# Inverses of 32x32 blocks in a decoder step: rows split by parity over the partitions, 8x8 blocks apart

## The chip, the core and the metric

The kernel runs on one core of one Trainium2 chip. The metric is the device time of one execution in microseconds (us). The core has five engines with queues of their own, each of which starts its instructions in order: TensorE (PE, with its weight load PEld), VectorE (DVE), ScalarE (ACT), GpSimd (POOL), and SyncE (SP), which in this kernel issues nearly all DMAs. An instruction that waits holds up whatever stands behind it on its engine.

## The reference

One decoder layer is applied to a prompt of 512 tokens and to 8 sampled sequences of 8 tokens (64 tokens more; 576 columns in all). Two token mixers share one input projection: an SSD mixer and an RWKV-7 mixer with 16 heads of 64. The change lies in the second. What it computes, per head and token:

```python
def step(s, inp):
    r_t, w_t, k_t, v_t, kk_t, a_t = inp
    s_kk = jnp.einsum('bhvk,bhk->bhv', s, kk_t)
    s = (s * w_t[:, :, None, :] - s_kk[..., None] * (kk_t * a_t)[:, :, None, :]
         + v_t[..., None] * k_t[:, :, None, :])
    return s, jnp.einsum('bhvk,bhk->bhv', s, r_t)
```

After the mixers come the output projection, a SwiGLU block, a per-layer embedding and norms. All of it is large matrix products with 576 columns.

## The kernel before

**The chunked form.** The recurrence is evaluated in chunks of 64 tokens: 8 chunks of the prompt (g = 1 to 8), and one chunk g = 0 that holds the 64 sampled tokens as 8 independent blocks of 8. Inside a chunk the delta rule needs the inverse of a unit lower triangular 64x64 matrix (stored transposed, so upper) for each head. The 16 heads are worked in four quarters of four heads (`jj` = 0, 1 and `e` = 0, 1), one quarter after the other.

**One quarter** goes through these steps, each a function: `prep` (decay, keys; elementwise work on DVE, ACT and POOL), `start_states` and `gram` (products of keys, masked; the strictly triangular part is kept in the tile `Lst`), `bonus`, `decayed`, `solve`, `combine`, `chain` (a serial pass over the chunks, with the state handed from one to the next) and `head_norm`.

**`solve`** inverts the two 32x32 diagonal blocks (`z` = 0, 1) of every 64x64 matrix. Two blocks, two heads `e`, 9 chunks and two `jj` make 72 blocks. They go from `Lst` to DRAM (`Ld`, line 669) and come back with one block on each of 72 partitions (`L`, line 672). DVE starts `Tt` as identity minus `L` (lines 674 and 675). Then 30 steps, each one product into `tmp` (line 681) and one subtraction (line 683), substitute column after column over all rows that are reached so far. A transposed copy (line 684) of the first half goes to `Ad`, and `Tt` to `Td` (lines 685 and 686).

**`combine`** loads `Td` into `TT` and `Ad` into `AA`, and makes the off-diagonal 32x32 block with two rounds of 64 small matmuls (lines 705 and 719). `chain` uses `TT`.

**What sets the order.** The functions are written one after the other, and a scheduler then gives each engine one fixed order by its own estimates. It lays independent work of other stages into the long serial ones: the input projections ("fills", lines 228 to 230; each loads weights as `raw` tiles in a ring of three, line 206, and splits them into `whi` on ACT and `wlo` on POOL and DVE in turn), and the chain of the previous quarter, which runs beside the solve of the next. So a solve has beside it on DVE the elementwise part of projections (lines 375 to 378), every other `wlo` (line 213) and the steps of the previous quarter's chain (lines 799, 812, 838).

Of the kernel before, what the change touches and what calls it, by code (L numbers as in the profile page):

```python
# [75 lines left out]
def hybrid_step(ctx, tc, A):  # L76
    nc = tc.nc
# [14 lines left out]
    def act(out, in_, func=AF.Copy, scale=1.0, bias=0.0):
        return S.activation(out, in_, func, bias=bias, scale=scale)  # L93
# [559 lines left out]
    def decayed(s):  # L653

        for jj in jj2:
            t = s.BK[jj][:, 1:9].rearrange("p g a t -> p g (a t)")
            G.tensor_tensor(t, t, s.PC[:, jj, 8:16].unsqueeze(2).to_broadcast([P, 8, P]), ALU.mult)

    def solve(s):

# [1 line left out]
        Ld = dp.tile([2, 2, 18, 32, 32], F32, tag=f"Ld{q}", name=f"Ld{q}")
        s.Td = dp.tile([2, 2, 18, 32, 32], F32, tag=f"Td{q}", name=f"Td{q}")
        s.Ad = dp.tile([2, 18, 32, 32], F32, tag=f"Ad{q}", name=f"Ad{q}")
        NB = 72
        for z in range(2):
            for e in range(2):
                r0 = e * 64 + z * 32
                nc.sync.dma_start(Ld[z, e].rearrange("g s t -> s g t"),
                                  s.Lst[r0:r0 + 32, :, :, z * 32:z * 32 + 32].rearrange("s g j t -> s (g j) t"))  # L670
        L = sp.tile([NB, 32, 32], F32, tag="L", name=nm("L"))
        nc.sync.dma_start(L[:], Ld[:].rearrange("z e g s t -> (z e g) s t"))
        Tt = s2.tile([NB, 32, 32], F32, tag="Tt", name=nm("Tt"))
        V.tensor_scalar(Tt[:], L[:], -1.0, None, ALU.mult)
        V.tensor_tensor(Tt[:].rearrange("p s t -> p (s t)")[:, 0:1024:33],
                        Tt[:].rearrange("p s t -> p (s t)")[:, 0:1024:33], ones[0:NB, 0:32], ALU.add)
        tmp = s2.tile([NB, 256], F32, tag="tmp", name=nm("tmp"))
        for jx in range(1, 31):
            n = 31 - jx
            o = tmp[:, 0:jx * n].rearrange("p (s t) -> p s t", s=jx)  # L680
            V.tensor_tensor(o, L[:, jx:jx + 1, jx + 1:32].to_broadcast([NB, jx, n]),  # L681
                            Tt[:, 0:jx, jx:jx + 1].to_broadcast([NB, jx, n]), ALU.mult)
            V.tensor_tensor(Tt[:, 0:jx, jx + 1:32], Tt[:, 0:jx, jx + 1:32], o, ALU.subtract)  # L683
        V.tensor_copy(L[0:36], Tt[0:36].rearrange("p s t -> p t s"))
        nc.sync.dma_start(s.Td[:].rearrange("z e g s t -> (z e g) s t"), Tt[:])
        nc.sync.dma_start(s.Ad[:].rearrange("e g s t -> (e g) s t"), L[0:36])

    def combine(s):

        TT = s.TT = inverses[s.q % 2]  # L690
        AA = s2.tile([P, 9, 2, 32], F32, tag="AA", name=nm("AA"))
        for e in range(2):
            for z in range(2):
                r0 = e * 64 + z * 32
                nc.sync.dma_start(TT[r0:r0 + 32, :, :, z * 32:z * 32 + 32].rearrange("s g j t -> s (g j) t"),
                                  s.Td[z, e].rearrange("g s t -> s g t"))
# [4 lines left out]
        for g in range(1, 9):
            for jj in jj2:
                for e in range(2):
                    lo_, hi_ = e * 64, e * 64 + 32
                    marks["c", s.q] = T.matmul(Wv[hi_:hi_ + 32, g - 1, jj, :], s.Lst[lo_:lo_ + 32, g, jj, 32:64],
                                               AA[lo_:lo_ + 32, g, jj, :], start=True, stop=True)
        for e in range(2):
            hi_ = e * 64 + 32
            if e:
                act(AA[hi_:hi_ + 32, 1:9], Wv[hi_:hi_ + 32], scale=-1.0)  # L710
            else:
                V.tensor_scalar(AA[hi_:hi_ + 32, 1:9], Wv[hi_:hi_ + 32], -1.0, None, ALU.mult)
# [1034 lines left out]
```

## Time and profile before

| | before |
|---|---|
| median of 3 runs | 1334.37 us (1331.13 to 1338.24) |
| the profiled execution | 1329.48 us, of which 1327.7 us are the span from its first to its last instruction |
| mean granted TensorE clock | 0.951 |
| instructions | 26629 |
| HBM read, written | 106.10 MB, 27.75 MB |

A row of a group of instructions gives the line, engine and operation, the tiles written and read, the shapes, the count, the busy time in us and the mean of one in ns, then the idle time of the engine ahead of them and what ended it. A row of the timeline gives start and duration in us. A row of a stretch of time gives the busy us of PE, PEld, DVE, ACT and POOL, each with its number of instructions, then the granted clock, the DMA share and GB/s. Line numbers are those of the kernel before; after the diff they stand 37 higher from `combine` on.

### The profile page before, as it was taken

To read this page: it belongs to the slowest core of one execution; us is meant where nothing else is said; L and a number is where in the kernel's file an instruction comes from. 1 tells how busy PE (TensorE), PEld (TensorE's weight loads), DVE (VectorE), ACT (ScalarE), POOL (GpSimd) and SP (SyncE) were. 2 spreads that over 40 slices of the span, in tenths; PEclk is the share of its full clock that TensorE was granted. 3 is DMA by queue.
4 is the path that set the end of the run, shared out by engine and by line. 5 is a ranking of instruction groups with operands and counts; after the bars stand their busy time and mean duration, and the time that the engine had idled before them with its cause. 6 is when DMAs were issued, how large, how long until landed. Compare 5 with 4: busy or idle time off the path is not lost.

```text
span 1327.7 us, 26629 instructions
## 1 busy us (share of the span) xinstructions
PE 1224.9 (92%) x10429; PEld 1125.1 (85%) x10429; DVE 885.8 (67%) x1569; ACT 632.0 (48%) x1274; POOL 615.4 (46%) x584
## 2 busy tenths in 40 slices
PE   6897899999989978899989989999999999999997
PEld 5786797889968966788769878999999999999996
DVE  6649665878696876953456576858895138883464
ACT  6565436543654374343444364455553225553363
POOL 5426513642265136122445665647565345654642
PEclk9898999799978979979989989999999999999998
DMA  5322241334232322353454541253342224424322
GB/s 167 127 65 72 78 116 54 98 96 119 73 103 79 83 72 78 103 180 106 132 182 131 201 151 59 78 161 106 98 113 89 81 83 114 116 66 136 99 89 72
DMA packets 96764, 140.29 MB, mean 106 GB/s; under 512 B 34960, under 2 KB 39312, under 8 KB 96640
## 3 DMA queue, kind: packets, MB, share of 16 engines
q1 hardware_dynamic: 93760, 133.36, 32.6%
q0 software_dynamic: 2304, 4.72, 2.1%
q8 instruction: 82, 1.34, 0.4%
q10 hardware_dynamic: 576, 0.52, 0.1%
q14 instruction: 42, 0.34, 0.1%
HBM read 106.10 MB, written 27.75 MB: 101 GB/s over the span
## 4 chain that ended last, share of the span: by engine, by line
PE 58%; DVE 19%; ACT 6%; issue 6%; DMA 4%; POOL 3%; SPq 0%; DVEq 0%; ACTq 0%; POOLq 0%
PE lin L241 12%; PE lin L1432 11%; PE lin L228 6%; PE lin L230 6%; PE lin L229 6%; DVE h L402 2%; DVE wl L191 1%; DVE Tt L683 1%; DVE tmp L681 1%; DVE wlo L213 1%; PE lin L1577 1%; PE lin L1578 1%; PE lin L1579 1%; DVE suv L838 1%; DMA raw<-wts 1%
## 5 line engine op out<-in xcount | busy, mean ns | idle before, releaser
L213 POOL TENSOR_TENSOR wlo<-raw,whi 128x512 fp32r<-128x512 f32 (+1 forms) x92 | 125.8, 1368 | 303.6 <-ACT whi L93 235.0
L228 PE MATMUL lin<-xhi,whi 128*128 128x288 f32 (+1 forms) x784 | 242.1, 309 | 2.8 <-ACT whi L93 2.2
L230 PE MATMUL lin<-xhi,wlo 128*128 128x288 f32 (+1 forms) x784 | 240.2, 307 | 4.0 <-POOL wlo L213 2.3
L229 PE MATMUL lin<-xlo,whi 128*128 128x288 f32 (+1 forms) x784 | 239.6, 306 | 1.2 <-POOL xlo L191 1.1
L93 ACT ACTIVATE whi<-raw 128x512 fp32r<-128x512 f32 (+1 forms) x200 | 123.2, 616 | 211.0 <-PE lin L241 90.0
L228 PEld LDWEIGHTS lin<-xhi,whi 128*128 128x128 f32 (+1 forms) x784 | 149.5, 191 | 10.1 <-ACT whi L93 2.6
L230 PEld LDWEIGHTS lin<-xhi,wlo 128*128 128x128 f32 (+1 forms) x784 | 149.4, 191 | 7.9 <-POOL wlo L213 2.7
L229 PEld LDWEIGHTS lin<-xlo,whi 128*128 128x128 f32 (+1 forms) x784 | 149.4, 191 | 6.5 <-POOL xlo L191 2.4
L213 DVE TENSOR_TENSOR wlo<-raw,whi 128x512 fp32r<-128x512 f32 (+1 forms) x108 | 82.1, 761 | 74.2 <-PE lin L241 36.0
L1432 PE MATMUL lin<-T,wh 128*128 128x288 f32 x576 | 87.3, 296 | 2.0 <-DVE e L1477 1.3
L1432 PEld LDWEIGHTS lin<-T,wh 128*128 128x128 f32 x576 | 80.0, 189 | 3.2 <-DVE e L1477 1.6
L93 ACT ACTIVATE wh<-raw 128x512 fp32r<-128x512 f32 x72 | 45.1, 628 | 52.5 <-PE lin L1432 35.4
L191 POOL TENSOR_TENSOR wl<-raw,wh 128x512 fp32r<-128x512 f32 x36 | 57.3, 1592 | 11.7 <-ACT wh L93 6.2
L191 DVE TENSOR_TENSOR wl<-sw,wh 128x512 fp32r<-128x512 f32 x53 | 49.9, 941 | 9.3 <-ACT wh L93 5.2
L241 PE MATMUL lin<-ah,whi 128*128 128x288 f32 x352 | 54.7, 294 | 0.0
L241 PE MATMUL lin<-al,whi 128*128 128x288 f32 x352 | 54.4, 294 | 0.0
L241 PE MATMUL lin<-ah,wlo 128*128 128x288 f32 x352 | 54.2, 294 | 0.0
L681 DVE TENSOR_TENSOR tmp<-L,Tt 72x30 f32<-72x30 f32 (+14 forms) x120 | 49.9, 416 | 3.2
L1432 PE MATMUL lin<-T,wl 128*128 128x288 f32 x288 | 49.8, 297 | 0.6 <-DVE wl L191 0.6
L241 PEld LDWEIGHTS lin<-ah,whi 128*128 128x128 f32 x352 | 49.3, 188 | 0.0
L241 PEld LDWEIGHTS lin<-al,whi 128*128 128x128 f32 x352 | 49.2, 188 | 0.0
L241 PEld LDWEIGHTS lin<-ah,wlo 128*128 128x128 f32 x352 | 49.2, 188 | 0.0
(437 smaller groups left out, 3265.7 us busy)
## 6 DMA issues: line engine op xcount, KB each, us to landing
raw<-wts SPq DMA_DIRECT2D x271, 256.0 KB, 2.6
S<-s_wkv SPq DMA_DIRECT2D x8, 512.0 KB, 5.1
hd<-s_ssm SPq DMA_DIRECT2D x8, 512.0 KB, 4.6
o_ssm_s<-hd SPq DMA_DIRECT2D x8, 512.0 KB, 2.8
xbc_d<-E SPq DMA_DIRECT2D x12, 288.0 KB, 2.1
x<-xT SPq DMA_DIRECT2D x8, 288.0 KB
gate_d<-g SPq DMA_DIRECT2D x8, 288.0 KB, 2.5
bv_d<-rw SPq DMA_DIRECT2D x8, 288.0 KB
```

What stands on the lines that cost most here:

```text
L93: return S.activation(out, in_, func, bias=bias, scale=scale)
L191: eng.tensor_tensor(lo, src, hi.bitcast(F32), ALU.subtract)
L213: eng.tensor_tensor(lo[:, 0:n], raw[:, 0:n], hi[:, 0:n].bitcast(F32), ALU.subtract)
L228: T.matmul(ps[:, a:b], whi, xhi[:, a:b], start=first, stop=False)
L229: T.matmul(ps[:, a:b], whi, xlo[:, a:b], start=False, stop=False)
L230: T.matmul(ps[:, a:b], wlo, xhi[:, a:b], start=False, stop=last)
L241: T.matmul(ps[:, a:e], (hi, lo)[p][:, i * P:(i + 1) * P], xs[k + i][q][:, a:e], start=n == k + i == 0, stop=n == 2 and k + i == nk - 1, sk ...
L402: V.scalar_tensor_tensor(h[:], E[:, i:i + 600], w(i), h[:], ALU.mult, ALU.add)
L681: V.tensor_tensor(o, L[:, jx:jx + 1, jx + 1:32].to_broadcast([NB, jx, n]), Tt[:, 0:jx, jx:jx + 1].to_broadcast([NB, jx, n]), ALU.mult)
L683: V.tensor_tensor(Tt[:, 0:jx, jx + 1:32], Tt[:, 0:jx, jx + 1:32], o, ALU.subtract)
L838: V.scalar_tensor_tensor(dst, sv[h, jj, 0, e], PC[h, jj, 7 + g:8 + g], dw[h, jj], ALU.mult, ALU.add)
L1432: T.matmul(ps, (hi, lo)[p][:, k * P:(k + 1) * P], OPS[n][k][q], start=first and p == q == k == 0, stop=p == 1 and k == 3, skip_group_check ...
```

## The change

It is confined to `solve`, the loads of `combine` and a new function.

- The 64 blocks of the prompt's chunks go to the 128 partitions twice, by four DMAs instead of one: partitions 0 to 63 hold the even rows of the 64 inverses, partitions 64 to 127 the odd ones. Each half uses the rows 0, 2, 4, ... of its tile `Tt`. GpSimd sets `Tt` to zero and writes the ones of the diagonal; the identity-minus-`L` step on DVE is gone. The substitution has 31 steps instead of 30, and step `jx` works on `jx // 2 + 1` rows instead of `jx`, on 128 partitions instead of 72.
- The transposed copy is made in two halves, one on DVE and one on ACT, and ACT moves the odd rows beside the even ones before `Td` is written by two DMAs.
- The sampled chunk's blocks are block diagonal with blocks of 8x8. Their 32 blocks of 8x8 are loaded by 8 small DMAs, inverted on GpSimd by 14 instructions (`small_blocks`), and written into `Td` by 8 small DMAs. The rest of those places in `Td` is set to zero once, at the start, by 8 DMAs.
- A solve then issues 33 DMAs instead of 13.

```diff
+    inverse_d = [dp.tile([2, 18, 2, 32, 32], F32, tag=f"Td{q}", name=f"Td{q}") for q in range(4)]
+    zero = sp.tile([8, 1024], F32, tag="L", name=nm("zero"))
+    G.memset(zero[:], 0.0)
+    for d in inverse_d:
+        for z in range(2):
+            nc.sync.dma_start(d[z, 0:2].rearrange("g e s t -> (g e) (s t)"), zero[0:4])
...
-        L = sp.tile([NB, 32, 32], F32, tag="L", name=nm("L"))
-        nc.sync.dma_start(L[:], Ld[:].rearrange("z e g s t -> (z e g) s t"))
-        Tt = s2.tile([NB, 32, 32], F32, tag="Tt", name=nm("Tt"))
-        V.tensor_scalar(Tt[:], L[:], -1.0, None, ALU.mult)
-        V.tensor_tensor(Tt[:].rearrange("p s t -> p (s t)")[:, 0:1024:33],
-                        Tt[:].rearrange("p s t -> p (s t)")[:, 0:1024:33], ones[0:NB, 0:32], ALU.add)
-        tmp = s2.tile([NB, 256], F32, tag="tmp", name=nm("tmp"))
-        for jx in range(1, 31):
-            n = 31 - jx
-            o = tmp[:, 0:jx * n].rearrange("p (s t) -> p s t", s=jx)
-            V.tensor_tensor(o, L[:, jx:jx + 1, jx + 1:32].to_broadcast([NB, jx, n]),
-                            Tt[:, 0:jx, jx:jx + 1].to_broadcast([NB, jx, n]), ALU.mult)
-            V.tensor_tensor(Tt[:, 0:jx, jx + 1:32], Tt[:, 0:jx, jx + 1:32], o, ALU.subtract)
-        V.tensor_copy(L[0:36], Tt[0:36].rearrange("p s t -> p t s"))
-        nc.sync.dma_start(s.Td[:].rearrange("z e g s t -> (z e g) s t"), Tt[:])
-        nc.sync.dma_start(s.Ad[:].rearrange("e g s t -> (e g) s t"), L[0:36])
+        Tt = s2.tile([P, 32, 32], F32, tag="Tt", name=nm("Tt"))
+        flat = Tt.rearrange("p s t -> p (s t)")
+        G.memset(Tt[:, 0:32:2], 0.0)
+        for h in range(2):
+            G.memset(flat[H[h], h:1024:66], 1.0)
+        L = sp.tile([P, 32, 32], F32, tag="L", name=nm("L"))
+        for z in range(2):
+            for h in range(2):
+                r0 = h * 64 + z * 32
+                nc.sync.dma_start(L[r0:r0 + 32], Ld[z, 2:18].rearrange("g e s t -> (g e) s t"))
+        small_blocks(Ld, s.Td)
+        tmp = s2.tile([P, 256], F32, tag="tmp", name=nm("tmp"))
+        for jx in range(31):
+            m, n = jx // 2 + 1, 31 - jx
+            o = tmp[:, 0:m * n].rearrange("p (s t) -> p s t", s=m)
+            V.tensor_tensor(o, L[:, jx:jx + 1, jx + 1:32].to_broadcast([P, m, n]),
+                            Tt[:, 0:2 * m:2, jx:jx + 1].to_broadcast([P, m, n]), ALU.mult)
+            V.tensor_tensor(Tt[:, 0:2 * m:2, jx + 1:32], Tt[:, 0:2 * m:2, jx + 1:32], o, ALU.subtract)
+        V.tensor_copy(L[0:32, :, 0:32:2], Tt[0:32, 0:32:2].rearrange("p s t -> p t s"))
+        act(L[0:32, :, 1:32:2], Tt[64:96, 0:32:2].rearrange("p s t -> p t s"))
+        nc.sync.dma_start(s.Ad[:].rearrange("g e s t -> (g e) s t"), L[0:32])
+        act(Tt[0:64, 1:32:2], Tt[64:128, 0:32:2])
+        for z in range(2):
+            nc.sync.dma_start(s.Td[z, 2:18].rearrange("g e s t -> (g e) s t"), Tt[z * 32:z * 32 + 32])
+
+    def small_blocks(Ld, Td):
+        Ls, Ts, o = (sp.tile([32, 8, 8], F32, tag="sb", name=nm("sb"), bufs=3) for _ in range(3))
+        def moves(d, t, out):
+            for z in range(2):
+                for c in range(4):
+                    a = d[z, 0:2, :, c * 8:c * 8 + 8, c * 8:c * 8 + 8].rearrange("g e s t -> (g e) s t")
+                    b = t[z * 16 + c * 4:z * 16 + c * 4 + 4]
+                    nc.sync.dma_start(*((a, b) if out else (b, a)))
+        moves(Ld, Ls, False)
+        G.tensor_scalar(Ts[:], Ls[:], -1.0, None, ALU.mult)
+        d = Ts.rearrange("p s t -> p (s t)")[:, 0:64:9]
+        G.tensor_tensor(d, d, ones[0:32, 0:8], ALU.add)
+        for jx in range(1, 7):
+            m, n = jx, 7 - jx
+            w = o[:].rearrange("p s t -> p (s t)")[:, 0:m * n].rearrange("p (s t) -> p s t", s=m)
+            G.tensor_tensor(w, Ls[:, jx:jx + 1, jx + 1:8].to_broadcast([32, m, n]),
+                            Ts[:, 0:jx, jx:jx + 1].to_broadcast([32, m, n]), ALU.mult)
+            G.tensor_tensor(Ts[:, 0:jx, jx + 1:8], Ts[:, 0:jx, jx + 1:8], w, ALU.subtract)
+        moves(Td, Ts, True)
```

The scheduler's order changes with it. Three places matter. The first is SP at the start of the third solve. Here `bv_d` is the bonus on its way to DRAM, `raw` weights, `gb` the operands of the previous quarter's head norm. Before:

```order
L669 DMA Ld_4937<-Lst_4839 32x18x32 x4
L672 DMA L_4944<-Ld_4937 72x1024
L606 DMA bv_d_169<-rw_4197 128x576
L606 DMA bv_d_170<-rw_4265 128x576
L206 DMA raw_5727<-wts 128x512
L891 DMA gb_3766<-gate_d_144 128x576
L892 DMA gb_3766<-bv_d_168 128x576
L206 DMA raw_5765<-wts 128x512
```

In the changed kernel:

```order
L929 DMA gb_3862<-bv_d_168 128x576
L675 DMA Ld_5033<-Lst_4935 32x18x32 x4
L686 DMA L_5043<-Ld_5033 32x1024 x2
L606 DMA bv_d_169<-rw_4293 128x576
L606 DMA bv_d_170<-rw_4361 128x576
L711 DMA sb_5048<-Ld_5033 4x8x8 x8
L206 DMA raw_5864<-wts 128x512
L711 DMA Td_471<-sb_5049 4x8x8 x8
L206 DMA raw_5932<-wts 128x512
```

The loads of `gb` stand ahead of the solve instead of in it, and the 8x8 blocks' loads and stores stand between the weights (the second pair of `L` loads and a second `raw` behind the first are left out of the rows, since they read like their neighbours).

The second place is POOL in the first solve, where `sb` are the tiles of the 8x8 blocks and `cso`, `E` belong to a convolution. Before, and then changed:

```order
L641 TENSOR_TENSOR G_982<-G_982,gmask 128x4x128
L213 TENSOR_TENSOR wlo_2281<-raw_2278,whi_2280 128x512
L396 COPY cso_2195<-E_2196 128x3
L395 COPY cso_2195<-E_2196 128x24
L393 COPY E_2783<-cst_2780 128x8x3
L394 COPY E_2783<-cst_2780 128x3
L213 TENSOR_TENSOR wlo_2349<-raw_2346,whi_2348 128x512
```

```order
L714 TENSOR_SCALAR sb_1540<-sb_1539 32x64
L716 TENSOR_TENSOR sb_1540<-sb_1540,ones 32x8
L720 TENSOR_TENSOR sb_1541<-sb_1539,sb_1540 32x6
L213 TENSOR_TENSOR wlo_2336<-raw_2333,whi_2335 128x512
L722 TENSOR_TENSOR sb_1540<-sb_1540,sb_1541 32x6
L396 COPY cso_2250<-E_2251 128x3
L395 COPY cso_2250<-E_2251 128x24
L720 TENSOR_TENSOR sb_1541<-sb_1539,sb_1540 32x10
L722 TENSOR_TENSOR sb_1540<-sb_1540,sb_1541 32x2x5
```

The first `wlo` now stands behind three instructions that wait for the 8x8 blocks, and the second behind all fourteen.

The third place is DVE at the start of the third solve (`suv` are values of the chain, `rw` the bonus product that `bv_d` stores). Before, and then changed:

```order
L812 TENSOR_SCALAR suv_3541<-cx_3606 64x2x64
L674 TENSOR_SCALAR Tt_4946<-L_4944 72x1024
L605 TENSOR_TENSOR rw_4265<-lin_4930,rw_4401 128x576
L675 TENSOR_TENSOR Tt_4946<-Tt_4946,ones 72x32
L681 TENSOR_TENSOR tmp_4949<-L_4944,Tt_4946 72x30
```

```order
L605 TENSOR_TENSOR rw_4361<-lin_5026,rw_4497 128x576
L692 TENSOR_TENSOR tmp_5081<-L_5043,Tt_5039 128x31
L694 TENSOR_TENSOR Tt_5039<-Tt_5039,tmp_5081 128x31
L692 TENSOR_TENSOR tmp_5081<-L_5043,Tt_5039 128x30
L849 TENSOR_SCALAR suv_3720<-cx_3785 64x2x64
```

The second bonus product no longer stands behind an instruction that waits for `L`, and a value of the chain now does.

On PE the first matmul of `combine` stands, counted in matmuls of input projections from the program's start, behind 927, 1536, 2016 and 2208 of them in the four quarters before, and behind 881, 1447, 1974 and 2208 in the changed kernel. The last products of `bonus` stand behind 600, 1152, 1704 and 2016 in both. Of the previous quarter's chain, 3, 4 and 4 state updates (line 830) stood on PE behind the bonus of quarters 2, 3 and 4; now it is 2, 2 and 3.

More of the change, by code (lines that the diff above doesn't have):

```diff
@@ L657, in decayed @@
             G.tensor_tensor(t, t, s.PC[:, jj, 8:16].unsqueeze(2).to_broadcast([P, 8, P]), ALU.mult)
+    inverse_d = [dp.tile([2, 18, 2, 32, 32], F32, tag=f"Td{q}", name=f"Td{q}") for q in range(4)]
[4 more added lines that the diff above has]
+            nc.sync.dma_start(d[z, 0:2].rearrange("g e s t -> (g e) (s t)"), zero[0:4])
     def solve(s):
         q = s.q
[L662 to L665, printed above, removed]
+        Ld = dp.tile([2, 18, 2, 32, 32], F32, tag=f"Ld{q}", name=f"Ld{q}")
+        s.Td = inverse_d[q]
+        s.Ad = dp.tile([16, 2, 32, 32], F32, tag=f"Ad{q}", name=f"Ad{q}")
         for z in range(2):
@@ L668, in solve @@
                 r0 = e * 64 + z * 32
-                nc.sync.dma_start(Ld[z, e].rearrange("g s t -> s g t"),
+                nc.sync.dma_start(Ld[z, :, e].rearrange("g s t -> s g t"),
                                   s.Lst[r0:r0 + 32, :, :, z * 32:z * 32 + 32].rearrange("s g j t -> s (g j) t"))
-        L = sp.tile([NB, 32, 32], F32, tag="L", name=nm("L"))
-        nc.sync.dma_start(L[:], Ld[:].rearrange("z e g s t -> (z e g) s t"))
-        Tt = s2.tile([NB, 32, 32], F32, tag="Tt", name=nm("Tt"))
@@ L695, in combine @@
                 nc.sync.dma_start(TT[r0:r0 + 32, :, :, z * 32:z * 32 + 32].rearrange("s g j t -> s (g j) t"),
-                                  s.Td[z, e].rearrange("g s t -> s g t"))
-            nc.sync.dma_start(AA[e * 64:e * 64 + 32].rearrange("s g j t -> s (g j) t"),
-                              s.Ad[e].rearrange("g s t -> s g t"))
+                                  s.Td[z, :, e].rearrange("g s t -> s g t"))
+            nc.sync.dma_start(AA[e * 64:e * 64 + 32, 1:9].rearrange("s g j t -> s (g j) t"),
+                              s.Ad[:, e].rearrange("g s t -> s g t"))
         Wp = cx_ps()
```

## The prediction

> **What bounds the kernel now.** I read the page first: the busy shares, then the chain that ended last.
>
> ```profile
> PE 1224.9 (92%) x10429; PEld 1125.1 (85%) x10429; DVE 885.8 (67%) x1569; ACT 632.0 (48%) x1274; POOL 615.4 (46%) x584
> PE 58%; DVE 19%; ACT 6%; issue 6%; DMA 4%; POOL 3%; SPq 0%; DVEq 0%; ACTq 0%; POOLq 0%
> ```
>
> PE is the bound on average and has 1327.7 - 1224.9 = 103 us idle. That average hides the stages, so next come stretches of 20 us in the quarters' part (140 to 600 us).
>
> ```profile
> 160.00:180.00 20.00, 20.00 (x152) 20.00 (x151) 18.49 (x44) 8.43 (x16) 4.73 (x5) 1.00 0.30 91
> 300.00:320.00 20.00, 19.29 (x156) 17.93 (x155) 18.98 (x49) 5.60 (x15) 5.74 (x7) 1.00 0.28 85
> 380.00:400.00 20.00, 15.21 (x153) 11.80 (x153) 17.43 (x29) 11.56 (x26) 8.06 (x13) 0.60 0.31 110
> 480.00:500.00 20.00, 14.68 (x168) 11.12 (x162) 17.45 (x28) 14.23 (x28) 9.43 (x12) 0.66 0.09 31
> 540.00:560.00 20.00, 16.09 (x148) 14.35 (x147) 18.94 (x45) 6.41 (x15) 4.42 (x6) 0.95 0.35 119
> 560.00:580.00 20.00, 17.91 (x123) 14.67 (x122) 11.58 (x32) 7.86 (x16) 1.53 (x2) 0.71 0.36 88
> ```
>
> The first two lie in solves 1 and 2: DVE is busy 18.5 and 19.0 of 20, but PE is full too, with projections. A faster DVE alone buys nothing there. The next two lie in `prep` of quarters 3 and 4: PE loses 4.8 and 5.3 us and runs at 0.60 and 0.66 of its clock. The last two are solve 4, where PE loses 3.9 and 2.1 us and falls to 0.71. So the time to be won is idle PE outside solves 1 to 3, and in solve 4. Three rows of PE's timeline show what it waits for near a solve.
>
> ```profile
> 190.21 0.24 PE L705 MATMUL cx<-AA,Lst 32*32 32x32 f32 x2 [1.36 <-DMA AA<-Ad]
> 421.54 0.71 PE L796 MATMUL cx<-suv,G 128*128 128x128 f32 x2 [2.27 <-DVE suv L838]
> 557.32 0.71 PE L796 MATMUL cx<-suv,G 128*128 128x128 f32 x4 [2.86 <-DVE suv L838]
> ```
>
> Only the first waits for a solve itself. The others wait for the chain's values on a DVE that the solve occupies.
>
> **Part by part.** The DVE groups of the four solves:
>
> ```profile
> L681 DVE TENSOR_TENSOR tmp<-L,Tt 72x30 f32<-72x30 f32 (+14 forms) x120 | 49.9, 416 | 3.2
> L683 DVE TENSOR_TENSOR Tt<-Tt,tmp 72x30 f32<-72x30 f32 (+14 forms) x120 | 45.1, 376 | 3.5
> L674 DVE TENSOR_SCALAR Tt<-L 72x1024 f32<-72x1024 f32 x4 | 6.2, 1545 | 11.6 <-DMA L<-Ld 11.6
> L675 DVE TENSOR_TENSOR Tt<-Tt,ones 72x32 f32<-72x32 f32 x4 | 1.1, 282 | 0.1
> L684 DVE COPY L<-Tt 36x1024 f32<-36x1024 f32 x4 | 4.4, 1093 | 0.2
> ```
>
> *Substitution.* The groups mix lengths and stalls, so I price one instruction from pairs that start back to back:
>
> ```profile
> 181.00 0.22 DVE L681 TENSOR_TENSOR tmp<-L,Tt 72x58 f32<-72x58 f32 x1
> 181.25 0.22 DVE L683 TENSOR_TENSOR Tt<-Tt,tmp 72x58 f32<-72x58 f32 x1
> 161.47 0.41 DVE L683 TENSOR_TENSOR Tt<-Tt,tmp 72x238 f32<-72x238 f32 x1
> 161.91 0.41 DVE L681 TENSOR_TENSOR tmp<-L,Tt 72x240 f32<-72x240 f32 x1
> 162.35 1.38 DVE L683 TENSOR_TENSOR Tt<-Tt,tmp 72x240 f32<-72x240 f32 x1
> ```
>
> Start to start is 0.25 us at 58 elements and 0.44 at 238 (the last row is a stall, see below), so 0.19 + 0.00106 per element. Before, a solve has 60 instructions and twice the sum of jx(31-jx) = 4960 elements: 11.4 + 10.5 = 21.9 us. Now it is 62 instructions and twice 2856 elements: 11.8 + 6.1 = 17.8 us. **4.1 us less**; the halved rows cannot halve the time, because half of it is per instruction. The wider partitions are taken as free; no row shows this operation on 128.
>
> *Start and copy.* Lines 674 and 675 go: 1.55 + 0.28 = 1.8 us. The copy of 1.09 us becomes half on DVE, 0.55 saved, and half on ACT, with ACT's move of the odd rows behind it:
>
> ```profile
> L93 ACT ACTIVATE AA<-cx 32x512 f32<-32x512 f32 x4 | 2.4, 591 | 2.9 <-DVE AA L712 2.8
> ```
>
> Two such cost 1.2 us of an engine at 48%. The first runs beside DVE's half; the second delays only `Td`, needed after `Ad`. The next `whi` stands behind them: uncovered, up to 1.2 us of PE per solve. Together DVE is spared 4.1 + 1.8 + 0.5 = **6.4 us a solve**.
>
> *8x8 blocks on GpSimd.* Fourteen small instructions a solve; the nearest rows are
>
> ```profile
> L576 POOL COPY pc<-pb 128x8 f32<-128x8 f32 x8 | 2.0, 246 | 0.0
> L645 POOL TENSOR_TENSOR G<-G,dgmask 64x128 f32<-64x128 f32 x8 | 3.5, 433 | 4.4 <-ACT G L93 4.1
> L466 POOL MEMSET TT<- 128x1152 f32 x2 | 2.1, 1070 | 0.0
> ```
>
> so 14 x 0.25 = 3.4 us to 14 x 0.43 = 6.1 us of POOL; I take 3.4, the smaller shape being nearer. POOL has the room (4.73 busy of 20 in solve 1). But these run beside DVE's substitution, and that is not free:
>
> ```profile
> 181.69 1.29 POOL L213 TENSOR_TENSOR wlo<-raw,whi 128x512 fp32r<-128x512 f32 x1 [5.12 <-ACT whi L93]
> 181.51 0.21 DVE L681 TENSOR_TENSOR tmp<-L,Tt 72x30 f32<-72x30 f32 x1
> 181.75 1.30 DVE L683 TENSOR_TENSOR Tt<-Tt,tmp 72x30 f32<-72x30 f32 x1
> ```
>
> Beside a POOL product, a DVE instruction that otherwise takes 0.21 us took 1.30 and ended with it. If each small instruction holds DVE for its length, DVE pays 3.4 us a solve (0 to 6.1), and its gain shrinks from 6.4 to **3.0 us** (0.3 to 6.4). I take 3.0. The Trainium skill, "SBUF — State Buffer", section "Who interferes with whom", says a VectorE instruction with two SBUF inputs and a GpSimd instruction that reads SBUF exclude each other for a whole instruction; the trace agrees (1.30 against 0.21 us). By it the sum is the one above; without it DVE would gain all 6.4.
>
> *DMAs.* A solve issues 20 more, and `L` moves 512 KB in four pieces instead of 288 KB in one.
>
> ```profile
> 137.61 2.00 SPq L669 DMA_DIRECT2D Ld<-Lst  x4
> 141.33 0.35 SPq L672 DMA_DIRECT2D L<-Ld  x1
> 148.70 5.11 SPq L206 DMA_DIRECT2D raw<-wts  x2
> 417.44 1.47 DVE L674 TENSOR_SCALAR Tt<-L 72x1024 f32<-72x1024 f32 x1 [4.86 <-DMA L<-Ld]
> ```
>
> Four issues took 2.00 us, so 0.5 each: the four `L` start 1.5 us later in the last piece, and I take **L 1.5 us later** (0, if the pieces overlap fully, to 3, if bytes set it), during which DVE stands. The three further `L` and eight loads of 8x8 blocks take 5.5 us, within the 7.4 us between `L` and the next weights (141.33 to 148.70). The eight stores take 4 us and wait for POOL, with weights behind them; two `raw` tiles stand ahead. One tile feeds 24 matmuls:
>
> ```profile
> 168.30 0.30 PE L228 MATMUL lin<-xhi,whi 128*128 128x288 f32 x1
> 168.43 0.29 PE L229 MATMUL lin<-xlo,whi 128*128 128x288 f32 x1
> ```
>
> at 0.133 us from start to start, so two last 6.4 us. POOL's 3.4 plus SP's 4 is 7.4: covered but for about 1 us, which the ring's third tile hides. I cost it at 0.5 us a solve (0 to 5). In the third solve the loads of `gb` no longer stand there.
>
> At the start, the memsets of `zero` (8x1024) and of the first `Tt` (128x512) put some 1.5 us by line 466 ahead of the first `wlo` on POOL, and eight DMAs on SP: **+1 us** (0 to 3).
>
> *What PE gets of it.* A solve's end comes 3.0 - 1.5 = 1.5 us earlier for DVE's part, more where chain steps have moved out of it. `combine` stands 46, 89, 42 and 0 projection matmuls earlier on PE, 6.1, 11.9, 5.6 and 0 us. These are moved, not saved: they cover the idle of the next `prep`.
> - Quarter 1: PE waits longer at line 705 (1.36 us before, about 4 now, as 6.1 us of work left while DVE gained little), and fills later gaps. Net -1.
> - Quarters 2 and 3: one and two chain steps leave the full stretch. A step is some 20 matmuls; 156 of mixed kind fill 20 us (300 to 320), so 2.6 us a step: 2.6 and 5.1 us of PE. `prep` takes them into its 4.8 and 5.3 us of idle, where DVE (17.4 of 20) gets 1.7 us more per step but loses `combine`. I keep half and more: -2 and -3.5.
> - Quarter 4: of 6.0 us idle, and a clock of 0.71 over 20 us (up to 5.8 us more), DVE's 3.0 us come off directly, with 1.5 of clock: -4.5.
>
> Sum: -1 - 2 - 3.5 - 4.5 + 4 x 0.5 + 1 = **-8.0 us**. The profiled execution took 1329.48, so 1321.5 by it; the median shown is 4.9 higher, and I predict against the median: 1334.37 - 8.0 = **1326.4 us**.
>
> **Rivals.**
> - *A, hidden.* PE is full in the solves, so freed DVE time ends as waiting; steps moved into `prep` prolong it as much as they shorten the solve. For: 20.00 of 20 in solve 1, 17.4 on DVE in `prep`. Against: solve 4. Only half of quarter 4 remains against +3 of new cost: 1334.37 - 2 + 3 = 1335.
> - *B, slower.* The eight stores hold SP until GpSimd is done. By 0.43 us each and with DVE holding POOL in turn (as long again), 14 last 12 us; plus 4 of SP, less 6.4 of cover, weights come 9.6 us late, and the ring hides some 5: PE stops 4.6 us in each of four solves, 18.4 us in place of the 2 counted above: 1334.37 - 10 + 18.4 = 1342.8. It decides once GpSimd's fourteen outlast the cover by more than the ring's tile, 3.2 us, that is from about 5.6 us on.
> - *C, more.* DVE is not held, keeps 6.4 a solve, and `prep`, DVE-bound at 17.4 of 20, shortens by it: 3 x 3.4 further, and solve 4 without the fall to 0.71 some 4 more: 1326.4 - 14 = 1312. The Trainium skill, "TensorE: Matmul & The Clock Gate", Part 1, has the clock halve after about 3.4 us idle; the waits here (2.86 us at 557) are near it, so little may tip it.
>
> **How the numbers follow.** Forecast 0.46, own range 1318 to 1332; A 0.28; B 0.17; C 0.09. 0.5% is 6.7 us, about what a measurement can tell from no change: faster is below 1327.7, slower above 1341. Of the forecast 0.31 lies below 1327.7 and 0.15 within; C adds 0.09 and the low tail of A 0.04: faster 0.44. Of B 0.10 is slower, 0.07 within; the high tail of A gives 0.05 and the forecast's own upper bounds (DMA, POOL) 0.03, out of its 0.15: slower 0.18, same 0.38. The range takes in most of B and of C: 1311 to 1343.
>
> **What would show it.** Right: DVE's groups of the solves fall from 106.7 us to some 75 plus stalls; fourteen POOL rows of 0.25 us; `L` on DVE 1 to 2 us later; PE's wait at `combine` 1 longer; idle after 552 us halved. Wrong: SP waiting for POOL with PE idle on `whi` or `wlo` behind it (B); 20-us stretches of `prep` longer than before (A); DVE instructions beside the small POOL ones unstretched (C).

## The result, and the profile after

The changed kernel takes 1339.44 us (median of 17 executions, 1337.73 to 1343.8) against 1332.56 us before (17, 1327.98 to 1339.55): a ratio of 1.0055, with a 95% interval of 1.0041 to 1.0070. It is slower by 6.9 us; the forecast was 1326.4 us and faster.

The profiled executions lie further apart (1343.8 against 1329.48 us): that of the changed kernel was its slowest, that of before among its faster ones. About half of the 14.4 us between the two spans is therefore chance, and single stretches are read with that in mind.

The busy shares and the chain that ended last, on the page of the changed kernel, and its mean clock:

```profile
PE 1239.1 (92%) x10429; PEld 1138.8 (85%) x10429; DVE 861.1 (64%) x1569; ACT 638.6 (48%) x1282; POOL 627.8 (47%) x653
PE 58%; DVE 17%; ACT 5%; issue 4%; DMA 3%; POOL 2%; SPq 1%; DVEq 0%; POOLq 0%; ACTq 0%
```

```profile
core 0: 1342.1 us, clock 0.940
```

On the chain that ended last, PE's share is as it was (58%) and DVE's fell from 19 to 17%. DVE has 24.7 us less to do. Its groups of the solves fell from 106.7 to 79.0 us, 6.9 us a solve, where 6.4 had been worked out; its other work takes 3.0 us more. Yet PE, with the same 10429 matmuls, is busy 14.2 us longer. Its idle time is the same: 1342.1 - 1239.1 = 103.0 us, before 102.8. So in sum none of the difference is more waiting; PE ran more of its work at half clock: 163 us of the span, before 133, so 15 us more were lost. The medians of all executions agree: with a mean clock of 0.943 over 1339.4 us, 76 us are lost, and before (0.948, 1332.6 us, 115 executions) 69, 7 us apart, which is the difference in time.

The groups of the solves, on DVE and on GpSimd:

```profile
L694 DVE TENSOR_TENSOR Tt<-Tt,tmp 128x126 f32<-128x126 f32 (+22 forms) x124 | 38.6, 312 | 3.4
L692 DVE TENSOR_TENSOR tmp<-L,Tt 128x126 f32<-128x126 f32 (+22 forms) x124 | 37.9, 305 | 18.8 <-DMA L<-Ld 9.2 <-DMA sb<-Ld 6.1
L695 DVE COPY L<-Tt 32x512 f32<-32x512 f32 x4 | 2.5, 620 | 0.1
L720 POOL TENSOR_TENSOR sb<-sb,sb 32x6 f32<-32x6 f32 (+2 forms) x24 | 7.0, 291 | 1.4
L722 POOL TENSOR_TENSOR sb<-sb,sb 32x6 f32<-32x6 f32 (+2 forms) x24 | 6.1, 256 | 1.6
```

The substitution itself did what was meant. 19.1 us a solve (76.5 / 4) replace 23.8 us; the wait for `L` grew in three of the four. From the timelines of SP and DVE, in us:

| solve | first issue of `Ld` to first DVE step, before / after | to the transposed copy, before / after |
|---|---|---|
| 1 | 7.6 / 7.2 | 45.5 / 40.1 |
| 2 | 7.0 / 9.2 | 52.0 / 45.7 |
| 3 | 8.2 / 10.7 | 47.8 / 40.5 |
| 4 | 7.2 / 8.2 | 43.8 / 37.2 |

Every solve ends 5.3 to 7.3 us sooner after its start, and the kernel is slower all the same. The same six stretches of 20 us as in the prediction:

```profile
160.00:180.00 20.00, 20.00 (x152) 20.00 (x151) 16.12 (x48) 8.96 (x16) 4.32 (x5) 1.00 0.35 97
300.00:320.00 20.00, 20.00 (x183) 18.23 (x181) 19.09 (x54) 7.91 (x18) 4.05 (x9) 1.00 0.30 89
380.00:400.00 20.00, 16.58 (x137) 14.73 (x135) 18.13 (x29) 14.49 (x30) 9.56 (x16) 0.91 0.28 92
480.00:500.00 20.00, 16.99 (x249) 13.47 (x242) 13.79 (x27) 14.66 (x31) 5.94 (x8) 0.96 0.20 62
540.00:560.00 20.00, 19.00 (x165) 17.43 (x164) 15.12 (x46) 7.08 (x16) 7.56 (x20) 1.00 0.45 142
560.00:580.00 20.00, 14.76 (x116) 11.35 (x115) 15.13 (x47) 5.64 (x13) 1.84 (x3) 0.75 0.41 107
```

These rows look better than before (`prep` at 380 and 480 idles 3.4 and 3.0 us against 4.8 and 5.3, at a clock of 0.91 and 0.96). They mislead, because the program runs 7 to 15 us behind from 280 us on and the weak stretches have moved out of these windows. A better measure is when PE starts a given projection matmul, counted from the program's start on lines 228 to 230. Against before, the changed kernel starts number 1152 1.2 us earlier (at 246.9 us), number 1200 6.8 us later (288.6), number 1632 15.6 us later, number 2016 12.8 and number 2544 9.8 us later (702.5). The first loss lies between 1152 and 1200, a stretch that holds `gram` of quarter 2 and takes 41.7 us instead of 33.7. PE is idle for 6.6 us of it (before 3.2) and at half clock for 22.3 us (before 13.7), which loses 4.3 us more; the two together make up nearly all of the 8.0 us. PE's waits there for values of quarter 1's chain, before and then changed:

```profile
259.23 0.58 PE L804 MATMUL cx<-xs,TT 64*64 64x64 f32 x5 [0.54 <-DVE xs L799]
279.72 0.38 PE L804 MATMUL cx<-xs,TT 64*64 64x64 f32 x5 [2.37 <-DVE xs L799]
```

```profile
251.51 0.38 PE L841 MATMUL cx<-xs,TT 64*64 64x64 f32 x5 [1.06 <-DVE xs L836]
255.69 0.59 PE L867 MATMUL cx<-suv,bkt 128*64 128x64 f32 x6 [1.58 <-DVE suv L849]
285.89 0.38 PE L841 MATMUL cx<-xs,TT 64*64 64x64 f32 x5 [2.71 <-DVE xs L836]
```

The first two stand on PE ahead of products of `gram`, and DVE, from which the values come, is busy 9.6 of 10 us there. The clock record has 20.5 us at half clock in one piece, from 252.6 us on (before 13.7, from 250.9 on), which covers most of `gram`; the solve behind it begins at 274.64 us in place of 267.90. The wait of 1.58 us begins 1.5 us after the clock has fallen, so it can't be what starts this piece.

### The profile page after: what moved, and what is told of

Same layout as the page of the kernel before. It is cut to its first block, busy times and chain, and to the rows that moved or that the text cites. A ratio compares the mean times of both kernels' runs of the same rounds, so it can differ in the third digit from the quotient of the medians.

```text
span 1342.1 us, 26841 instructions
## 1 busy us (share of the span) xinstructions
PE 1239.1 (92%) x10429; PEld 1138.8 (85%) x10429; DVE 861.1 (64%) x1569; ACT 638.6 (48%) x1282; POOL 627.8 (47%) x653
## 4 chain that ended last, share of the span: by engine, by line
PE 58%; DVE 17%; ACT 5%; issue 4%; DMA 3%; POOL 2%; SPq 1%; DVEq 0%; POOLq 0%; ACTq 0%
PE lin L241 12%; PE lin L1469 10%; PE lin L228 6%; PE lin L230 6%; PE lin L229 6%; PE lin L620 2%; DVE Tt L694 2%; DVE wl L191 1%; DVE tmp L692 1%; DVE h L402 1%; PE lin L1614 1%; PE lin L1615 1%; PE lin L1616 1%; DVE wlo L213 1%; PE cx L833 1%
## 5 line engine op out<-in xcount | busy, mean ns | idle before, releaser
L228 PE MATMUL lin<-xhi,whi 128*128 128x288 f32 (+1 forms) x784 | 245.6, 314 | 4.9 <-ACT whi L93 2.2
L213 POOL TENSOR_TENSOR wlo<-raw,whi 128x512 fp32r<-128x512 f32 (+1 forms) x92 | 122.3, 1329 | 265.2 <-ACT whi L93 224.0
L692 DVE TENSOR_TENSOR tmp<-L,Tt 128x126 f32<-128x126 f32 (+22 forms) x124 | 37.9, 305 | 18.8 <-DMA L<-Ld 9.2
L230 PE MATMUL lin<-xu,wlo 128*128 128x288 f32 x128 | 40.3, 316 | 10.0 <-DVE wlo L213 5.5
```

Of the source, the lines that this page charges most:

```text
L213: eng.tensor_tensor(lo[:, 0:n], raw[:, 0:n], hi[:, 0:n].bitcast(F32), ALU.subtract)
L228: T.matmul(ps[:, a:b], whi, xhi[:, a:b], start=first, stop=False)
L230: T.matmul(ps[:, a:b], wlo, xhi[:, a:b], start=False, stop=last)
```

## The experiments

Eighteen kernels were run, each with before on the same chip. Half clock is the sum of such pieces in the clock record of the one profile. The last column is the start of matmuls 1200 and 2544 against before (281.80 and 692.61 us), also of that profile. The expectations speak of the former as matmul 1248, a count that set 48 too many ahead of it. One profile need not be typical of its kernel: that of held_q1 is its fastest execution (1335.6 us, median 1343.9), that of half_rows_held its slowest (1338.3 us, median 1332.5).

| kernel | ratio to before (95%) | half clock, us | 1200 / 2544, us |
|---|---|---|---|
| before | 1 | 133 | 0 / 0 |
| changed | 1.0055 (1.0041 to 1.0070) | 163 | +6.8 / +9.8 |
| no_small | 1.0055 (1.0033 to 1.0078) | 154 | +8.1 / +9.4 |
| half_rows | 1.0088 (1.0053 to 1.0123) | 178 | +10.2 / +10.8 |
| small_added | 0.9999 (0.9976 to 1.0022) | 136 | -1.0 / 0.0 |
| zero_late | 1.0040 (1.0021 to 1.0060) | 177 | +9.3 / +8.4 |
| held_all | 1.0018 (0.9996 to 1.0040) | 129 | -2.6 / -4.4 |
| half_rows_held | 1.0000 (0.9977 to 1.0022) | 147 | -3.2 / +4.7 |
| held_q2_q3 | 1.0066 (1.0045 to 1.0087) | 153 | +7.6 / +8.3 |
| held_q3 | 1.0062 (1.0041 to 1.0082) | 161 | +7.8 / +12.8 |
| held_q1 | 1.0076 (1.0047 to 1.0106) | 141 | -2.7 / +4.5 |
| held_later | 1.0091 (1.0067 to 1.0114) | 157 | +1.0 / +14.4 |
| before_later | 1.0044 (1.0029 to 1.0060) | 158 | +1.9 / +6.3 |
| warm | 1.0133 (1.0107 to 1.0158) | 161 | +0.1 / +14.8 |
| warm_same_order | 1.0070 (1.0043 to 1.0096) | 161 | -1.1 / +3.3 |
| held_warm | 1.0096 (1.0071 to 1.0120) | 141 | -3.9 / +13.2 |
| before_warm4 | 1.0114 (1.0094 to 1.0133) | 147 | +2.9 / +14.3 |
| before_warm1 | 0.9987 (0.9965 to 1.0008) | 134 | -0.2 / +1.5 |
| no_steps_held | 0.9948 (0.9929 to 0.9968) | 116 | -3.5 / -10.6 |
| held_warm1 | 0.9998 (0.9980 to 1.0016) | 138 | -3.1 / -0.6 |

### The parts of the change, one at a time

**no_small**: the changed kernel without its 8x8 blocks.

```diff
-        small_blocks(Ld, s.Td)
```

> The changed kernel without its 8x8 blocks: the call of small_blocks is left out (16 DMAs and 14 GpSimd instructions a solve), so the sampled chunk's inverses stay zero; the rest, and the order of PE around combine (881, 1447, 1974, 2208 projection matmuls ahead of the four), is as in the changed kernel. Theory 'order' (the cheaper substitution puts combine and the chain earlier, which moves PE's idle and lengthens its time at half clock; the small blocks are hidden): 1336 to 1340 us, +3 to +7 against before. Theory 'added work' (the DMAs and GpSimd instructions of the small blocks hold SP, the weights and DVE): 1324 to 1332 us, at or under before.

1341.1 us, the ratio of the changed kernel. The GpSimd work and the sixteen DMAs are not the loss.

**half_rows**: the kernel before with shorter steps and nothing else.

```diff
-            n = 31 - jx
+            m, n = jx // 2 + 1, 31 - jx
-            o = tmp[:, 0:jx * n]
+            o = tmp[:, 0:m * n]
```

(and `m` for `jx` in the rows of both instructions)

> The kernel before with nothing of the change but fewer elements: each substitution step works on jx // 2 + 1 rows in place of jx, on the same 72 partitions (the other rows are left out, so the inverses are wrong). No further DMA, no GpSimd work, no memset. PE's order by this is nearly that of the changed kernel (885, 1447, 1962, 2208 projection matmuls ahead of the combines; before 927, 1536, 2016, 2208). Theory 'order': slower than before all the same, +3 to +7 us. Theory 'added work': the DVE gain is real and shows, -5 to -10 us against before.

1347.4 us: with less work on DVE, and no new work anywhere, the kernel is slower still than the changed one.

```profile
core 0: 1345.9 us, clock 0.935
```

**small_added**: the kernel before and `small_blocks` on top of it.

```diff
+        small_blocks(Ld, Sd)
         Tt = s2.tile([NB, 32, 32], F32, tag="Tt", name=nm("Tt"))
```

> The kernel before, with the whole 32x32 substitution on DVE as it was, and small_blocks in addition (16 DMAs and 14 GpSimd instructions a solve, results stored to a tensor that nobody reads; Ld, Td and Ad have the group ahead of e). PE's order is that of before (927, 1536, 2016, 2208). Theory 'order': 0 to +2 us against before. Theory 'added work': +6 to +10 us against before.

1331.9 us, a ratio of 0.9999. With no_small this settles the added work from both sides: it is hidden.

**zero_late**: the clearing of `Td` moved from the start to behind `decayed` of quarter 1.

```diff
         decayed(s)
+        if s.q == 0:
+            clear()
```

(`clear` holds the memset of `zero` and the eight stores)

> The changed kernel with the memset of zero and its eight stores behind decayed of the first quarter in place of the program's start. PE's order nearly as in the changed kernel (881, 1447, 1968, 2208). If the start costs what the first 60 us show (1.0 us later after 192 projection matmuls): -0.5 to -1 us against the changed kernel. Theories 'order' and 'added work' both leave the rest of the loss: 1337 to 1340 us. If the eight stores at the start were the loss, 1332 us.

1338.2 us. Its interval overlaps that of the changed kernel. In the traces the first 1 us does not go with the memset either: matmul 192 starts 1.0 us late in the changed kernel, 0.3 in held_all, which has the memset at the start too, and 1.1 in half_rows_held, which hasn't.

So a cheaper substitution is what makes the kernel slower, and of the kernels so far, the four with combine at some 881 and 1447 matmuls are the slow ones. The scheduler had used its own estimate of the shorter solve to put `combine` and the chain behind it earlier.

### The place of combine

An edge queues the first matmul of `combine` behind a given projection matmul; it is an order on PE and no wait.

```diff
+    for q, n in ((0, 927), (1, 1536), (2, 2016)):
+        tc.add_manual_dep(marks["c0", q].ins, MM[n - 1].ins.name, mybir.DependencyInfo(
+            mybir.DependencyClass.NoSync, mybir.DependencyReason.DATA), reason="hold")
```

(`MM` lists the projection matmuls, `marks["c0", q]` is the first matmul of `combine`)

**held_all**: the whole change, with the places of before.

> The changed kernel, whole, but the first matmul of combine is queued on PE behind the projection matmul behind which it stands in the kernel before: 927, 1536 and 2016 for quarters 1 to 3 (the fourth stands at 2208 in both). An order on one engine, no wait. Theory 'order': the loss goes, 1322 to 1333 us (0 to -10 against before), and the time at half clock falls from 163 us to about 135. Rival 'the new work itself' (no_small and half_rows spoke against its parts, not against L's later arrival together with the rest): 1337 to 1341, as the changed kernel.

1335.9 us, 1.0018 (0.9996 to 1.0040): most of the loss goes. Half clock is 129 us in this profile, which is of one of its faster executions (1332.5 us); over all twelve the mean clock (median 0.9465) leaves 71 us lost, against 76 in the changed kernel and 69 before. No gain over before appears. PE's waits of over 0.5 us on the chain and on `gram` between 230 and 268 us are now:

```profile
232.94 0.35 PE L836 MATMUL cx<-suv,G 128*128 128x128 f32 x1 [0.59 <-DVE suv L878]
247.91 0.58 PE L836 MATMUL cx<-suv,G 128*128 128x128 f32 x1 [0.88 <-DVE suv L878]
258.30 0.58 PE L622 MATMUL lin<-G,bk 64*128 64x128 f32 x2 [0.95 <-ACT G L93]
```

The piece of half clock in `gram` lasts 17.1 us here, longer than before (13.7), and matmul 1200 still starts 2.6 us earlier than before.

**half_rows_held**: half_rows with the same three edges.

> half_rows (the kernel before with half of the substitution's rows left out) with the same queueing of combine at 927, 1536 and 2016. half_rows gave 1347 us. Theory 'order': 1322 to 1332 us, what the cheaper substitution is worth by itself when nothing else moves. Rival 'a faster solve hurts however it is ordered' (the chain's DVE steps and POOL's products meet elsewhere): 1340 to 1348.

1332.5 us, 1.0000. The edges alone take away the 0.88% of half_rows: the loss is the order, which is shown here. And the 5.4 us that DVE saves in each solve by these shorter steps (95.0 - 73.5 = 21.5 us in four) are worth nothing that can be measured.

**held_q2_q3** and **held_q3**: only some quarters held, by `((1, 1536),)` and by `((2, 2016),)`.

```diff
-    for q, n in ((0, 927), (1, 1536), (2, 2016)):
+    for q, n in ((1, 1536),):
```

> The changed kernel with combine queued behind projection matmul 1536 in quarter 2 and, by the scheduler's own answer, behind 2016 in quarter 3; quarter 1 stays early (881, 884). Against held_all it tells what the early combine of quarter 1 costs. By the trace of the changed kernel the 8 us between matmul 1152 and matmul 1200 come behind the early combine of quarter 1: then 1330 to 1337, 5 to 8 over held_all.

> The changed kernel with combine queued behind projection matmul 2016 in quarter 3 alone (changed kernel: 1974); quarters 1 and 2 stay early (881, 1447). Against the changed kernel it tells what quarter 3 costs, against held_q2_q3 what quarter 2 costs. By the trace of the changed kernel quarter 3 costs nothing from its combine on (12.8 us behind at matmul 2016, 12.6 at 2208): 1337 to 1341.

1343.6 and 1340.9 us (1.0066 and 1.0062): as slow as the changed kernel, so with quarter 1 early, holding the others brings nothing. Over held_all, held_q2_q3 takes 7.7 us more, within the 5 to 8 that were expected, though not the time of 1330 to 1337 us.

**held_q1**, **held_later**, **before_later**: quarter 1 alone, `((0, 927),)`; later in quarter 1; and the kernel before with `((0, 1008),)`.

```diff
-    for q, n in ((0, 927), (1, 1536), (2, 2016)):
+    for q, n in ((0, 1008), (1, 1536), (2, 2016)):
```

> The changed kernel with combine queued behind projection matmul 927 in quarter 1 alone; the scheduler then puts quarter 2's at 1507 and quarter 3's at 2016 by itself. held_all gave 1335.9 us (1.0018), held_q2_q3 1343.6 (1.0066). If the early combine of quarter 1 is the whole of the loss: 1333 to 1338 us. If the loss is spread over the quarters: 1338 to 1342.

> The changed kernel with combine still later than before: behind projection matmuls 1008, 1536 and 2016 (held_all 927, 1536, 2016). If the time falls the later the chain of quarter 1 begins (the projections run ahead of it, and its steps no longer stand in PE's queue ahead of the products of gram): 1327 to 1334 us, a version that beats both. If 927 is a place that merely suits: 1336 to 1345.

> The kernel before with combine of quarter 1 queued behind projection matmul 1008 in place of 927 (quarters 2 and 3 come out at 1538 and 2016). With held_later it tells whether the place of combine or the change decides: theory 'order' has both move the same way against held_all and before, within 3 us. 1326 to 1340 us.

These went against the theory. held_q1 gives 1343.9 us, with six executions spread from 1335.6 to 1345.9, so quarter 1 is needed but isn't the whole. Later places lose as well: 1345.7 us and, without any part of the change, 1339.4 us. The clock isn't what makes held_later slow: its median is 0.947, which leaves 71 us lost, while the kernel before lost 72 on the same chip and took 11.5 us less. "Earlier is worse" falls. What holds is that the time depends on where `combine` stands, by up to 0.9%, and that the places of before are the best of those tried.

### The clock

**warm**: sixteen further matmuls of constants in `gram` of quarter 2, ahead of two of the waits.

```diff
+        def warm(g, ps):
+            if q == 0 and g in WARM:
+                for _ in range(8):
+                    with tc.issue_after(marks[q, g].ins):
+                        marks[q, g] = T.matmul(ps[:, 0:128], cen[:], ident[:], start=True, stop=True)
```

> The changed kernel with two times eight 128x128 matmuls of constants in step 4 of quarter 1's chain, which lies in gram of quarter 2: one set ahead of the products that wait for xs, one ahead of those that wait for suv (1.06 and 1.58 us of idle PE in the changed kernel, at 251 and 255 us); their results are overwritten. Combine of quarters 2 and 3 comes out at 1491 and 1994 (changed kernel 1447, 1974), so the stretch up to matmul 1248 is what counts. If those two waits start the 20.5 us at half clock: half clock begins later or is shorter by 3.4 to 7 us there, and matmul 1248 comes 1 to 3 us sooner than in the changed kernel (289 us). If the small products of gram themselves bring the clock down: half clock as before, matmul 1248 0 to 2 us later.

The half clock there fell from 20.5 to 6.8 us, and matmul 1200 started 6.7 us sooner than in the changed kernel, more than expected; so the clock in that stretch can be had. It does not tell what brings the clock down, since the sets both stand in the waits and put larger products among the small ones. But `combine` of quarters 2 and 3 moved, and the kernel took 1350.6 us.

**warm_same_order**: the same, with edges in both directions that keep `combine` where the changed kernel has it.

```diff
+    for q, n in ((0, 881), (1, 1447), (2, 1974)):
+        for x, y in ((marks["c0", q], MM[n - 1]), (MM[n], marks["c0", q])):
+            tc.add_manual_dep(x.ins, y.ins.name, mybir.DependencyInfo(
```

> The changed kernel with the two sets of eight matmuls of constants of warm (step 4 of quarter 1's chain), and combine kept where the changed kernel has it (881, 1447; 1980 in place of 1974 in quarter 3), which warm had not (1491, 1994). In warm the half clock in gram of quarter 2 fell from 20.5 to 6.8 us and matmul 1248 came 6.7 us sooner, but later stages lost it again. If the half clock that PE's waits start there carries a part of the loss to the end of the program: 1331 to 1337 us, time at half clock 163 us less 10 to 20. If what is won there is only passed on to a later wait: 1338 to 1342, time at half clock as in the changed kernel. If the sets cost more than they win: over 1342.

Three stretches of 10 us of the changed kernel, and the same of this one:

```profile
250.00:260.00 10.00, 6.85 (x82) 5.67 (x81) 9.63 (x17) 5.33 (x11) 5.46 (x6) 0.63 0.12 30
260.00:270.00 10.00, 10.00 (x78) 7.99 (x76) 3.97 (x13) 4.23 (x13) 5.38 (x11) 0.50 0.10 33
270.00:280.00 10.00, 10.00 (x88) 8.53 (x87) 4.65 (x12) 4.68 (x14) 9.11 (x10) 0.84 0.43 103
```

```profile
250.00:260.00 10.00, 8.21 (x101) 7.38 (x98) 8.81 (x14) 4.25 (x7) 4.75 (x6) 0.66 0.11 35
260.00:270.00 10.00, 8.55 (x113) 7.03 (x114) 6.07 (x19) 7.53 (x22) 7.65 (x13) 1.00 0.10 29
270.00:280.00 10.00, 9.80 (x87) 8.69 (x86) 4.26 (x10) 3.27 (x10) 8.24 (x9) 1.00 0.69 187
```

From 260 to 270 us PE runs 113 matmuls in 8.55 busy us at full clock, in place of 78 in 10.00 at half. Matmul 1200 starts 7.9 us sooner, matmul 2544 still 6.5 us sooner, and the span is 2.5 us shorter; by the medians (1341.3 us against 1339.4) nothing is won. Half clock is 161 us as before the sets: what left `gram` of quarter 2 came back in later pieces. In the changed kernel the clock is where the time goes, but mending one place doesn't bring it back.

**held_warm**, **before_warm4**, **before_warm1**, **held_warm1**: such sets with `combine` in before's places, at four points (pairs of quarter, counted from 0, and step of its chain) or at one.

```diff
-    WARM = ((0, 4),)
+    WARM = ((0, 4), (1, 2), (1, 3), (2, 1))
```

> held_all (the changed kernel, combine at 927, 1536, 2016; 1335.9 us) with such sets at four places where its PE waits ahead of a half clock: step 4 of quarter 1's chain, steps 2 and 3 of quarter 2's, step 1 of quarter 3's. Theory 'clock': half clock 129 us falls to 100 to 115, time 1324 to 1332. If the sets (about 2 us each at full clock, eight of them) only take PE's time: 1338 to 1350.

> The kernel before (combine queued at the places it has) with the same four places of such sets. Theory 'clock': half clock 133 us falls to 105 to 120, time 1321 to 1330, so that waits and clock, and not the inverses, are what a change has to touch here. If the sets only take PE's time: 1336 to 1348.

> The kernel before (combine where it has it) with two sets at the one place, step 4 of quarter 1's chain. Theory 'clock': the 13.7 us at half clock at 262 us fall to 3.4 to 7, time 1327 to 1331. If not: 1333 to 1337.

> held_all (the changed kernel with combine at 927, 1536, 2016; 1335.9 us, 1.0018) with the two sets of constant matmuls in step 4 of quarter 1's chain alone. before_warm1 gained 0.3% or less against held in the same manner (0.9987 of before, interval to 1.0008). If both small gains add: 1326 to 1331. If what is won there is passed on: 1332 to 1338.

Four points cost more than they win (1342.9 and 1346.0 us). One point gives 1331.0 us and, with the change, 1333.5 us: 0.9987 and 0.9998, both intervals with 1 in them. In before_warm1 the piece of half clock in `gram` of quarter 2 falls from 13.7 to 6.8 us, and the sum of such pieces stays (134 us, before 133). (The 262 us in its expectation is 250.9 us from the span's start.) No version that beats both kernels came of it.

**no_steps_held**: the bound from the other side.

```diff
-        for jx in range(1, 31):
+        for jx in range(1, 2):
```

> The kernel before with combine queued behind 927, 1536 and 2016 as it was, and 29 of the 30 substitution steps left out (only step 1 stays, so the inverses are wrong): some 21 us of DVE less in each solve, five times what the change can save. If DVE's time in the solves is hidden behind PE's projections and the previous chain: 1326 to 1334 us. If it counts once the order stands: half of 4 x 21 us or more in quarters 2 to 4, 1290 to 1315.

1325.1 us, 0.9948. Its page:

```profile
PE 1217.0 (92%) x10429; PEld 1119.4 (85%) x10429; DVE 802.1 (61%) x1337; ACT 633.2 (48%) x1274; POOL 612.3 (46%) x584
```

DVE loses 885.8 - 802.1 = 83.7 us, and the kernel 7.2 us (1332.35 to 1325.13): 0.09 us for each us. At that rate, an estimate, the 24.7 us that the change saves are worth 2 us, less than the new order costs.

## Why the prediction was wrong

**What held.** The substitution: 4.1 us less a solve were forecast, 4.6 measured (18.5 / 4). The start (7.3 / 4 = 1.8 us) and the copy (1.9 / 4 = 0.5) went as worked out. `L` was forecast 1.5 us later; it was -0.5, 2.2, 2.5 and 1.0 us. The eight stores held nothing up (small_added 0.9999), so rival B is out. The memsets and stores at the start, put at 1 us, show as 0.3 us at matmul 600; zero_late shows no cost of them that is clear of noise.

**A term that was mis-sized.** DVE was to be held by GpSimd's small instructions for 3.4 us a solve. Its groups of the solves fell by 6.9 us each, more than the 6.4 us worked out without any hold, and of the 43 substitution instructions that ran beside nothing else on GpSimd than these, none took more than 0.04 us over the median of its shape; so what "SBUF — State Buffer" of the Trainium skill says in "Who interferes with whom" (the two exclude each other for a whole instruction) did not show as lost time beside instructions as short as these, and the measurement decides. By rival C's condition that should have been worth 14 us more; it was worth nothing, since the term it feeds failed.

**The step that failed.** It is the one that turned DVE's time into PE's: "`combine` stands 46, 89, 42 and 0 projection matmuls earlier on PE [...] These are moved, not saved: they cover the idle of the next `prep`", and the gains of 1, 2 and 3.5 us for quarters 1 to 3 worked out from it. What the runs show in its place:
- The matmuls moved, but the chain's steps came forward with them, into a stretch where DVE is full, and stand on PE ahead of `gram`. They wait there (1.06 and 1.58 us), and PE's clock is halved for longer. With `combine` put back, the loss is 0.18% or nothing (held_all, half_rows_held). So the new order costs some 5 us (1.0055 against 1.0018) to 12 us (1.0088 against 1.0000), where a gain of 6.5 was forecast. That the order costs this is shown; that it does so by these waits and this piece of half clock is not, since warm_same_order took most of that half clock back, started matmul 1200 7.9 us sooner, and was no faster.
- The prediction had the sign of that effect as zero or positive, because it read the order's shift as more cover for later. The chance of a pure change of order to lose was in no rival: A priced it at nothing ("prolong it as much as they shorten the solve").
- DVE's time in the solves is nearly hidden behind PE even in the order of before: 84 us less of it gave 7 us (no_steps_held).

**Quarter 4**, put at -4.5, failed for another reason: "DVE's 3.0 us come off directly". There the order did not change (2208 in both), and the solve was 6.6 us shorter, but PE doesn't wait for it:

```profile
571.89 0.58 PE L841 MATMUL cx<-xs,TT 64*64 64x64 f32 x5 [3.41 <-DVE xs L836]
593.86 0.64 PE L813 MATMUL tr<-ident,bk 128*128 128x128 f32 x2 [3.00 <-ACT bkt L93]
596.12 0.58 PE L742 MATMUL cx<-AA,Lst 32*32 32x32 f32 x14
```

The copy of solve 4 started at 573.5 us, and `combine` on PE at 596.1, without any wait for `AA`. Ahead of it in PE's queue stand the last chain step of quarter 3, its head norm and the first transposes of quarter 4's own chain (line 813), and those are what waits. In the kernel before it was so too: copy at 567.9 us, `combine` at 583.0, again with no wait. There the last load of `AA` was issued at 573.45 us; by the median of 2.5 us from issue to landing it was there at about 576, an estimate, so this solve's end had some 7 us of slack, and bringing it forward only adds to the slack; a look at what stands ahead of `combine` there would have shown it.

**PE's wait at combine of quarter 1** was to grow from 1.36 to about 4 us; it was 1.09, because the solve shortened by 5.3 us and not by 1.5.

**The rivals.** With the order held, A is what the runs show: hidden. no_steps_held gives its size, 0.09 us per us of DVE.

**What stays open.** Why the places 927, 1536 and 2016 suit and neighbours to both sides don't is not settled. In the changed kernel and half_rows the time lost to half clock grew as the time did (76 and 82 us by the medians, before 69), in held_later it did not; and warm_same_order took 14 us of half clock from one place and found it again elsewhere. Nor does one profile of each resolve it: the stretch from matmul 2544 to the end, which none of these kernels touches, took between 635.1 us (before) and 643.7 us.

## What to carry to other kernels

A cheaper stage changes the fixed order of every engine when a scheduler works from estimates, and that order can cost more than the stage saves; rerun the old order with the new code before judging either, and, if it can be had, the new order with the old code (here it was not run; half_rows, the old code with work cut out, is the nearest). Ask of a stage first what the kernel would gain if it took no time at all: one run with the steps left out gave 7 us for 84 us of DVE, and in that order a faster version of the steps can hardly give more. And compare busy time and clock beside idle time: two profiled executions with 103 us of idle PE each differed by 14 us.

## What the hardware showed

The pieces of half clock in the records come in multiples of 3.41 us (from 3.41 to 27.3); only the last piece of a profile, at the program's end, is cut off between. In the kernel before, 15 of the 16 pieces start after 1.2 to 2.8 us of PE idle within the 3.41 us ahead of them. The other one is that of `gram` of quarter 2, which starts at 250.9 us although PE was busy throughout the 10 us ahead:

```profile
248.33 1.22 PE L741 MATMUL cb<-G,S 64*64 64x16 f32 x34
249.74 1.10 PE L741 MATMUL cb<-G,S 64*64 64x16 f32 x30
245.00:250.00 5.00, 5.00 (x79) 4.29 (x78) 4.92 (x9) 3.60 (x6) 0.73 (x2) 1.00 0.29 102
250.00:255.00 5.00, 5.00 (x55) 4.07 (x52) 4.81 (x9) 3.27 (x9) 4.75 (x5) 0.59 0.26 71
```

In the 2.6 us up to the fall, nearly all that PE ran was the 64 small products of the first two rows. In the changed kernel too PE was busy 10.00 of 10 us in `gram` with small products and stayed at half clock; sixteen more 128x128 matmuls ahead of that stretch brought it back to full after 6.8 us. That the size of the products decides is argued from these rows and was not tested apart from the waits. The Trainium skill, "TensorE: Matmul & The Clock Gate", Part 1, which the prediction drew on, has the clock halve after about 3.4 us without work; in the kernel before it halved after 1.2 to 2.8 us of idle PE, and once after none, so the measurement decides.

GpSimd's instructions on 32 partitions and up to 12 elements took 0.20 us at the median (seven of all 56 small ones took 0.60 to 0.79), and beside them no substitution instruction of DVE took more than 0.04 us over the median of its shape.
